# One decoder step on one core: merge loads in rows, matmuls in fours, early sample queries, and seven gates computed ahead

## The chip, the cores and the metric

The kernel runs on one core of one Trainium2 chip, as one program launched once. The metric is the device time in microseconds; lower is better. A core has five engines that run their own instruction streams and wait for each other through semaphores: TensorE (PE, with weight loads shown apart as PEld), VectorE (DVE), ScalarE (ACT), GpSimd (POOL) and SyncE (SP), which in this kernel issues every DMA.

## The reference

One inference step of one decoder layer, for a prompt of 512 tokens and for 8 sample sequences of 4 new tokens each (32 sample tokens; 544 token columns in all), width 1024, everything in float32:

```python
gate, (qa, ka, va, za, qkv_b, zb, a_b, b_b, ga, gb) = layer_front(x, c, w_cond, b_cond, w_in)
# branch A: dilated sliding-window softmax attention, 3 head groups, (window, dilation) =
# (128,1), (512,4), (2048,16), 8 heads of 64 each; the groups' outputs are combined with
# weights = softmax over their log-sum-exp
o_a = combine_groups(outs, lses)
# branch B: causal conv of width 4, silu, l2-normed q and k, gated delta rule in chunks
state, o_b = delta_branch(qkv_ext, a_b, b_b, state0, conv_w, a_log, dt_bias)
# layer_back
ya = o_a.reshape(bsz, seq, A_OUT_WIDTH).astype(dtype) * jax.nn.silu(za)
ob = ob * lax.rsqrt(jnp.mean(ob * ob, axis=-1, keepdims=True) + NORM_EPS) * b_norm_w
yb = ob.reshape(bsz, seq, B_WIDTH).astype(dtype) * jax.nn.silu(zb)
merged = jax.nn.sigmoid(ga) * (ya @ w_branch_a) + jax.nn.sigmoid(gb) * (yb @ w_branch_b)
r = (ALPHA * x + gate[:, None] * (merged @ w_out)).astype(jnp.float32)
# then LayerNorm over each row of r
```

The sample tokens attend to caches of 128, 512 and 2048 positions per sequence. The outputs are both results, the new caches (nearly all of their bytes are copied from the old caches by DMA), the conv states and the delta states.

## The kernel before, in words

**Tiles.** The whole input projection is done in column tiles of 128 output columns. One tile is a *job*: for each half of the 544 token columns (272), 8 blocks of the contraction times three matmuls `hi*hi`, `hi*lo`, `lo*hi`, because every float32 operand is split into a rounded part and a rest. So a job of 8 blocks is 48 matmuls of 128 by 128 by 272. ACT makes `hi` of a weight tile, DVE makes `lo`. Weight tiles are loaded by SP into `wraw` (three buffers), split into `wsp` (two buffers each), and results go to two PSUM banks `pp`. Branch A's output product (`w_ga`) has 4 blocks, so 24 matmuls per job.

**Order of the jobs.** First 60 jobs for the projections of conv/delta-rule heads and attention; then `za_job` 0 to 3 (the gate of branch A's four 128-column groups), `zb_job` 0 to 7 (the gate of branch B's eight heads); then for each of 8 columns `gate_job("gb")` and `branch_job("gb")`, then two `gate_job("ga")`; then for each of 8 columns the rest of `gate_job("ga")` and `branch_job("ga")` with `merge_after`, and last the product with `w_out` and the LayerNorm, five row tiles in two column halves.

**Beside the jobs.** `delta_blocks` and `delta_rule` handle the eight heads of branch B, `prompt_attention` handles the four groups j of branch A. After each odd j it does the *merge*: it gathers the softmax statistics by matmuls into a PSUM bank that another matmul has filled with ones, computes weights `R`, stores `R` to DRAM (`dw`), loads rows of it back broadcast over 64 partitions (`wv`), and for each of two groups multiplies `ya` and `NB` by their weights and adds them. The `wv` tiles use the two buffers of the tag `PT`. For j = 1 these six operations per merge run on POOL (`ce = ge`), for j = 3 on DVE. `sample_attention` is called twice: the early one (`T` = 0) streams its keys and values through nine tiles of the pool `op` (the tag `o`), called `slab`; the late one (`T` = 1) streams through `s2` tiles called `kv`. Each multiplies key tiles by the query rows `qr` and reduces them on DVE, then the same with values. `qr` is made by transposing the sample queries, storing them to DRAM (`qd`) and loading them back in another shape. `sample_delta` updates the sample states. `gate_rows` multiplies the conditioning vector by the last third of `w_cond` and spreads it to `gp` and `gs`, which the last stage multiplies with.

**What sets the order.** The body only records operations with a rank. `schedule()` then simulates the five engines with a table of costs and writes out a fixed order for each engine (list scheduling: lowest rank first among those ready). PE operations of the jobs have rank 9, the last; the jobs' other operations have rank -1, the first. Tiles of a pool are handed out in the order of recording, a tile is handed on when its last operation has been placed, and a pool can only be opened when those before it on its side have been closed, which needs every operation on them placed. Every engine then executes its list strictly in order and waits where an operand isn't there yet. The copies of the caches (`moves`, 168 DMAs of half a megabyte) have due times in that simulation from 48 to 850 us, on SP's list like all other DMAs.

**Pools that matter here.** `ap` holds attention's tiles (`P`, `PT`, `NB`, `spare`, `wv`), `dl` the delta rule's. `zp` (tiles `zt` and `rbo` of `zb_job` and of the gates) opens only after `ap` and `dl` have been closed, so after the last merge and the last head of the delta rule. `op` has 9 tiles: slabs, then `nd`, then the eight `ybh` of branch B, then the four `yal` of branch A. The pool `al` (`gp`, `gs`, `wo`) and `wcp` (the last third of `w_cond`) open after the late sample attention is over.

Of the kernel before, what the change touches and what calls it, by code (L numbers as in the profile page):

```python
# [37 lines left out]
MOVES = (48.0, 850.0)  # L38
S0B = 7
# [203 lines left out]
class Recorder:  # L243
# [439 lines left out]
def body(ctx, tc, io):  # L683
# [49 lines left out]
    bnw = consts.tile([128, 1], F32, name="bnw")  # L733
    hbnw = consts.tile([128, 1], F32, name="hbnw")
    eps4 = consts.tile([128, 1], F32, name="eps4")
    ve.memset(eps4, 4.0 * NORM_EPS)
    eps1 = consts.tile([128, 1], F32, name="eps1")
# [15 lines left out]
    hmask = keep.tile([128, 4], F32, name="hmask")  # L753

# [572 lines left out]
    dw = dram.tile([2, 128, 2, 128], F32, name="dw")  # L1327
# [32 lines left out]
    def prompt_attention():  # L1360

        for j in range(4):
# [95 lines left out]
            pe.matmul(pt, ones[0:1, :], ones[0:1, None, :].to_broadcast([1, 4, 128]), start=True, stop=True)  # L1458
# [20 lines left out]
            sp.dma_start(dw[j // 2], R[:, 0:2])  # L1479
            ce = ve if j == 3 else ge  # L1480
            for j2 in (j - 1, j):
                wv = []
                for u in range(2):
                    w = ap.tile([128, 512], F32, name="wv", tag="PT", bufs=2)
                    for hh in range(2):
                        h4 = 2 * (j2 % 2) + hh
                        sp.dma_start(w[64 * hh:64 * hh + 64].rearrange("p (r c) -> p r c", r=4),
                                     dw[j // 2, h4:128:32, u, :][None].to_broadcast([64, 4, 128]))
                    wv.append(w.rearrange("p (r a n) -> p r a n", r=4, a=4))
                time = lambda t: t[:, :SEQ].rearrange("p (n a r) -> p r a n", a=4, r=4)  # L1490
                ce.tensor_mul(time(ya[j2]), time(ya[j2]), wv[0])
                ce.tensor_mul(time(NB[:, j2 % 2]), time(NB[:, j2 % 2]), wv[1])
                ce.tensor_add(ya[j2][:, :SEQ], ya[j2][:, :SEQ], NB[:, j2 % 2])
                threads.set(merged[j2], 0.0)
# [55 lines left out]

    def sample_attention(T, t, stream, W, pace_of, by, over):
# [11 lines left out]
        qn = stream()[0:64, 0:256]  # L1563
        for jl in range(2):
            j = 2 * T + jl
            pt = pg()
            pe.transpose(pt[0:96, 0:128], ks[:, j].rearrange("p g n -> p (g n)"), ident)
            pe.transpose(pt[0:96, 128:256], vs[:, j].rearrange("p g n -> p (g n)"), ident)
            pe.transpose(pt[0:64, 256:384], qs[:, j, 1:3].rearrange("p g n -> p (g n)"), ident)
            ve.tensor_copy(knv[:, :, 128 * jl:128 * jl + 128], pt[0:96, 0:256].rearrange("p (u c) -> p u c", u=2))  # L1570
            se.activation(qn[:, 128 * jl:128 * jl + 128], pt[0:64, 256:384], AF.Copy)
        sp.dma_start(qd[T].rearrange("g t c -> (g t) c"), qn)

        qr = t["qr"].rearrange("p (g d) -> p g d", g=2)
        sp.dma_start(qr, qd[T].rearrange("g t (h d) -> (t h) g d", d=64))
# [81 lines left out]
        for x, vt in enumerate(vts):  # L1657
            for y in range(m):
                bp, bl = (m * x + y) // 2, (m * x + y) % 2
                o = pO[32 * bp:32 * bp + 32, 0:256]  # L1660
# [3 lines left out]
                pe.matmul(o, PTa[:, 128 * bl + 32 * bp:128 * bl + 32 * bp + 32], vt[:, 256 * y:256 * y + 256],  # L1664
                          start=False, stop=(bl == 1), tile_position=(0, 32 * bp))
# [24 lines left out]
    def early_tiles():  # L1690

        slab = [op.tile([128, NT], F32, name="slab", tag="o") for _ in range(9)]
        t = {}
        for i, names in ((4, ("Sa", "qr")), (5, ("Sb", "od", "o2")), (6, ("sba", "PTn")), (7, ("sbb", "om")), (8, ("knv",))):
# [4 lines left out]
        for n in ("Qz", "PTa", "sst"):  # L1699
# [135 lines left out]
    def zb_job(h):  # L1835
# [3 lines left out]
        def begin():  # L1839
            t["rows"] = zp.tile([128, SEQ], F32, name="rbo")  # L1840
            sp.dma_start(t["rows"], dO[h])

        def evac(n, ps):
            if not n:
                t["zt"] = zp.tile([128, NT], F32, name="zt")
# [4 lines left out]
        def after():  # L1850
# [9 lines left out]
        return column_job(("zb", h), evac=evac, begin=begin, after=after)  # L1860
# [11 lines left out]
    def gate_job(s, m):  # L1872

        def evac(n, ps):
            if not n:
                gate_tile[s, m] = zp.tile([128, NT], F32, name="zt")
# [17 lines left out]
    def gate_rows():  # L1894

        def load(part):
            for n in range(2):
                for k in range(0, KT, 2):
                    wc = wcp.tile([128, 2, 512], F32, name="wc")
                    sp.dma_start(wc, cond_rows(part, k, 2)[:, :, 512 * n:512 * n + 512])  # L1900
                    yield k, n, wc[:, 0]
                    yield k + 1, n, wc[:, 1]

# [5 lines left out]
        for _ in cond_product(2, load, ps):  # L1909
            yield 1.0  # L1910
# [21 lines left out]
    jobs += [za_job(j) for j in range(4)] + [zb_job(h) for h in range(8)]  # L1932
# [12 lines left out]
    threads.add(stream(60 + 4), 9)  # L1945
# [9 lines left out]
    def early():  # L1955
        yield freed[1], merged[1]
        yield from sample_attention(0, *early_tiles(), 512, 6.0, (ve,), early_over)
# [23 lines left out]
    def samples():  # L1981
# [3 lines left out]
        yield from sample_attention(1, {n: s1.tile([128, w], F32, name=n) for n, w in SHAPES.items()},  # L1985
# [12 lines left out]
    jobs += [gate_job("ga", m) for m in range(2)]  # L1998
# [44 lines left out]
    for m in range(8):  # L2043
        jobs += [gate_job("ga", m)] * (m > 1) + [branch_job("ga", m, 4, of_a, after=merge_after(m))]
# [188 lines left out]
```

## Time and profile before

| | |
|---|---|
| time, median of 3 runs | 1012.84 us |
| the three runs | 1013.37, 1012.84, 1010.07 us |
| the profiled execution's own time | 1010.26 us |
| its span, first to last instruction | 1008.3 us |
| TensorE clock granted, mean over the span | 0.973 |
| ACT busy | 418.4 us (41%) |
| POOL busy | 80.1 us (8%) |
| DMA read and written | 220.40 MB and 103.93 MB |

All of the kernel's arithmetic is recorded through one helper, so every row says line 630; rows are told apart by tile names (`pp<-hhi,hi` is a matmul of a job into its PSUM bank, `lo<-wt,hi` the split of a weight tile on DVE). A PE row's duration includes the pipeline's depth, so matmuls that follow each other every 0.125 us show 0.29 us each. "Idle before" counts only time in which that engine did nothing.

### The profile page before, as it was taken

Reading aid. Unit: us, or ns where it says so; the run is one execution under the profiler, and the core shown is the slowest. Engines: PE = TensorE matmul, PEld = TensorE weight load, DVE = VectorE, ACT = ScalarE, POOL = GpSimd, SP = SyncE. Lnnn points to the kernel's source line nnn. Section 1 sums busy time; section 2 is a strip of 40 time slices with the busy share of each in tenths; the row PEclk is TensorE's granted clock in tenths of the full one; section 3 lists DMA queues with packets and bytes.
Section 4 is the critical chain, followed back from the end, with each engine's and each line's share of the span. In section 5 each row is a group of like instructions: output and inputs, shape, how many; then the busy total and the mean of one; then the engine's idle time right before and its main releaser. Section 6 shows DMA issues by size and latency. Waiting matters only on the chain.

```text
span 1008.3 us, 20686 instructions
## 1 busy us (share of the span) xinstructions
PE 939.0 (93%) x8074; PEld 850.1 (84%) x8074; DVE 736.7 (73%) x1612; ACT 418.4 (41%) x975; POOL 80.1 (8%) x182
## 2 busy tenths in 40 slices
PE   4899999999999989999999999959999999799896
PEld 1699989999889988878898988848999998578785
DVE  0574576767599888989998776447978999546468
ACT  0364348444565443557434564223332221225220
POOL 0120001100102600011000101010010000000000
PEclk9899999999999999999999999879999999799998
DMA  9677755676787888857778474496889999824312
GB/s 361 194 243 226 228 176 202 203 242 182 219 272 259 264 274 272 288 189 247 244 278 280 155 221 151 138 283 254 275 263 392 422 394 328 308 85 135 130 56 108
DMA packets 109605, 237.98 MB, mean 236 GB/s; under 512 B 30899, under 2 KB 66429, under 8 KB 106821
## 3 DMA queue, kind: packets, MB, share of 16 engines
q1 hardware_dynamic: 109508, 236.68, 69.9%
q8 instruction: 63, 1.03, 0.4%
q14 instruction: 34, 0.27, 0.1%
HBM read 220.40 MB, written 103.93 MB: 322 GB/s over the span
## 4 chain that ended last, share of the span: by engine, by line
PE 47%; DVE 20%; DMA 6%; issue 3%; ACT 2%; POOL 0%; SPq 0%; DVEq 0%; ACTq 0%; POOLq 0%
PE pp L630 35%; PE pg L630 6%; PE pd L630 5%; DVE lo L630 2%; DVE r L630 2%; DVE slab L630 2%; DMA wv<-dw 2%; DVE acc L630 2%; PE pb L630 1%; DVE tmp L630 1%; DVE Tb L630 1%; DVE NTs L630 1%; DMA slab<-in_ks 1%; DMA wt<-in_w_in 1%; ACT hi L630 1%
## 5 line engine op out<-in xcount | busy, mean ns | idle before, releaser
L630 PE MATMUL pp<-hhi,hi 128*128 128x272 f32 x1408 | 416.1, 296 | 14.3 <-DVE zt L630 10.7
L630 PE MATMUL pp<-hhi,lo 128*128 128x272 f32 x1408 | 415.7, 296 | 0.6 <-DVE lo L630 0.6
L630 PE MATMUL pp<-hlo,hi 128*128 128x272 f32 x1408 | 413.7, 294 | 1.4 <-DVE hlo L630 1.4
L630 PEld LDWEIGHTS pp<-hhi,hi 128*128 128x128 f32 x1408 | 269.4, 191 | 18.8 <-DVE zt L630 11.2
L630 PEld LDWEIGHTS pp<-hlo,hi 128*128 128x128 f32 x1408 | 269.5, 191 | 5.1 <-issue 2.6
L630 PEld LDWEIGHTS pp<-hhi,lo 128*128 128x128 f32 x1408 | 269.2, 191 | 3.9 <-issue 1.9
L630 ACT ACTIVATE hi<-wt 128x1024 fp32r<-128x1024 f32 (+1 forms) x104 | 106.7, 1026 | 180.6 <-PE pp L630 164.2
L630 DVE TENSOR_TENSOR lo<-wt,hi 128x1024 fp32r<-128x1024 f32 (+1 forms) x104 | 124.1, 1193 | 66.4 <-ACT hi L630 65.9
L630 DVE SCALAR_TENSOR_TENSOR acc<-ext,cw,acc 128x568 f32<-128x568 f32 x72 | 57.5, 799 | 1.3 <-ACT ecum L630 0.8
L630 ACT ACT_TABLE_LOAD x38 | 48.8, 1283 | 13.9 <-DMA cT<-in_cT 7.8
L630 DVE TENSOR_TENSOR slab<-slab 128x512 f32<-128x512 f32 (+1 forms) x66 | 43.7, 676 | 3.1 <-DMA slab<-in_ks 2.6
L630 DVE TENSOR_REDUCE slab<-slab 128x8 f32<-128x512 f32 (+1 forms) x64 | 42.5, 674 | 0.3
L630 ACT ACTIVATE P<-P,st 128x256 f32<-128x256 f32 (+1 forms) x64 | 31.3, 490 | 24.5 <-DVE st L630 24.1
L630 ACT ACTIVATE zt<-pp 128x272 f32<-128x272 f32 x48 | 18.5, 388 | 52.9 <-PE pp L630 38.7
L630 PE MATMUL pp<-ybl,hi 128*128 128x272 f32 x128 | 37.1, 290 | 0.0
L630 PE MATMUL pp<-ybh,hi 128*128 128x272 f32 x128 | 36.8, 287 | 0.0
L630 PE MATMUL pp<-ybh,lo 128*128 128x272 f32 x128 | 36.8, 287 | 0.0
L630 PE MATMUL pg<-k,q 64*128 64x128 f32 (+1 forms) x192 | 33.3, 329 | 1.9 <-DVE st L630 1.9
L630 POOL COPY cx<-ext 128x3 f32<-128x3 f32 (+1 forms) x48 | 26.7, 586 | 84.2 <-ACT ext L630 84.2
L630 DVE SCALAR_TENSOR_TENSOR zt<-zt,pp 128x272 f32<-128x272 f32 x32 | 13.7, 433 | 26.1 <-PE pp L630 20.6
L630 PEld LDWEIGHTS pg<-k,q 64*128 64x128 f32 x192 | 22.4, 186 | 9.0 <-issue 3.6
L630 DVE CUSTOM_DVE_ANT_0 P<-pg,bias 128x256 f32<-128x256 f32 (+1 forms) x64 | 24.3, 400 | 7.4 <-PE pg L630 7.1
(398 smaller groups left out, 1617.0 us busy)
## 6 DMA issues: line engine op xcount, KB each, us to landing
out_kv_s<-in_cache SPq DMA_DIRECT2D x144, 512.0 KB
wt<-in_w_in SPq DMA_DIRECT2D x88, 512.0 KB
out_kv_s<-in_cache SPq DMA_DIRECT2D x24, 496.0 KB
wc<-in_w_cond SPq DMA_DIRECT2D x8, 1024.0 KB
slab<-in_ks SPq DMA_DIRECT2D x32, 256.0 KB
slab<-in_vs SPq DMA_DIRECT2D x32, 256.0 KB
kv<-in_ks SPq DMA_DIRECT2D x16, 512.0 KB
kv<-in_vs SPq DMA_DIRECT2D x16, 512.0 KB
```

The source lines that it names most:

```text
L630: getattr(real[x.engine], x.name)(*map(arg, x.args), **{k: arg(v) for k, v in x.kw.items()})
```

## The change

1. **Merge.** The bank of ones is written by DVE (`memset`) and not by a matmul. `R` goes to `dw` with four DMAs of four partitions each, so that a head's 512 weights lie in one row; each `wv` load then reads 2 KB rows and not 512-byte pieces. The second group's `wv` tiles take the two buffers of the tag `P`, not the same two as the first group's. The arithmetic of both merges runs on DVE.
2. **Orders in fours.** In `schedule()`, the first operation of a group recorded `together` now waits for all that any operation of the group needs from outside. The matmuls of the sample attention's last product are recorded in such a group, by fours in four different column strips of PE; those of `gate_rows` in groups of four contraction blocks with their loads recorded in front.
3. **Early sample queries.** `sample_queries` (transposes, copies, store and load of `qd`) is taken out of `sample_attention`. For `T` = 0 it is called right before; for `T` = 1 it is called at the end of the early thread, once the last attention inputs are there, into the kept tile `qr1`. Four one-column tiles become one, and `sst` moves to a slab, which makes room for `qr1`.
4. **Gates ahead.** `zb_job` 0 and 1 are put between `za_job` 1 and 2, with their `zt` in `op` tiles; the rest of their work (`finish`: the rows from DRAM, transposes, scaling, split) is done at the beginning of the next stage by `finish_early`. And `gate_job("ga")` 2 to 6 are added behind 0 and 1, ahead of the end of the stage, with `zt` in `op` tiles.

```diff
+EARLY_A, EARLY_B = 7, 2
...
+        for op in ops:
+            if op.group is not None and op.n != op.group[0]:
+                for d, data in op.deps.items():
+                    if d < op.group[0]:
+                        first = ops[op.group[0]].deps
+                        first[d] = first.get(d, False) or data
...
-    dw = dram.tile([2, 128, 2, 128], F32, name="dw")
+    dw = dram.tile([2, 4, 2, 4, 128], F32, name="dw")
...
-            pe.matmul(pt, ones[0:1, :], ones[0:1, None, :].to_broadcast([1, 4, 128]), start=True, stop=True)
+            ve.memset(pt, 1.0)
...
-            sp.dma_start(dw[j // 2], R[:, 0:2])
-            ce = ve if j == 3 else ge
+            for r in range(4):
+                sp.dma_start(dw[j // 2, :, :, r, :], R[32 * r:32 * r + 4, 0:2])
...
-                    w = ap.tile([128, 512], F32, name="wv", tag="PT", bufs=2)
+                    w = ap.tile([128, 512], F32, name="wv", tag="PT" if j2 < j else "P", bufs=2)
                     for hh in range(2):
-                        h4 = 2 * (j2 % 2) + hh
-                        sp.dma_start(w[64 * hh:64 * hh + 64].rearrange("p (r c) -> p r c", r=4),
-                                     dw[j // 2, h4:128:32, u, :][None].to_broadcast([64, 4, 128]))
+                        src = dw[j // 2, 2 * (j2 % 2) + hh, u].rearrange("r c -> (r c)")
+                        sp.dma_start(w[64 * hh:64 * hh + 64], src[None, :].to_broadcast([64, 512]))
...
+    def sample_queries(T, qn, qr):
+
+        for jl in range(2):
+            pt = pg()
+            pe.transpose(pt[0:64, 0:128], qs[:, 2 * T + jl, 1:3].rearrange("p g n -> p (g n)"), ident)
+            se.activation(qn[:, 128 * jl:128 * jl + 128], pt[0:64, 0:128], AF.Copy)
+        sp.dma_start(qd[T].rearrange("g t c -> (g t) c"), qn)
+        sp.dma_start(qr.rearrange("p (g d) -> p g d", g=2), qd[T].rearrange("g t (h d) -> (t h) g d", d=64))
...
+        with rec.together():
+            for bp in range(4):
                 bs = slice(32 * bp, 32 * bp + 32)
-                if not bl:
-                    pe.matmul(o, PTn[0:96, bs], knv[:, 1, :], start=True, stop=False, tile_position=(0, 32 * bp))
...
+                t["zt"] = op.tile([128, NT], F32, name="zt", tag="o") if early else zp.tile([128, NT], F32, name="zt")
...
+        if early:
+            unfinished.append((rows, finish))
+            return column_job(("zb", h), evac=evac)
+        return column_job(("zb", h), evac=evac, begin=rows, after=finish)
+
+    def finish_early():
+        for rows, finish in unfinished:
+            rows()
+            yield 3.0
+            finish()
...
+                far = s == "ga" and 2 <= m < EARLY_A
+                gate_tile[s, m] = op.tile([128, NT], F32, name="zt", tag="o") if far else zp.tile([128, NT], F32, name="zt")
...
+            for k0 in range(0, KT, 4):
+                wc = []
+                for k in (k0, k0 + 2):
+                    wc.append(wcp.tile([128, 2, 512], F32, name="wc"))
+                    sp.dma_start(wc[-1], cond_rows(2, k, 2)[:, :, w])
+                with rec.together():
+                    take(cond_product(2, lambda part: ((k0 + k, n, wc[k // 2][:, k % 2]) for k in range(4)), ps), 99)
+                yield 2.0
...
-    jobs += [za_job(j) for j in range(4)] + [zb_job(h) for h in range(8)]
+    jobs += [za_job(j) for j in range(2)] + [zb_job(h, True) for h in range(EARLY_B)] + [za_job(j) for j in range(2, 4)]
+    jobs += [zb_job(h) for h in range(EARLY_B, 8)]
...
+        t, slabs = early_tiles()
+        sample_queries(0, slabs()[0:64, 0:256], t["qr"])
+        yield from sample_attention(0, t, slabs, 512, 6.0, (ve,), early_over)
+        yield tuple(ready[3, g] for g in range(3))
+        sample_queries(1, slabs()[0:64, 0:256], qr1)
...
-    jobs += [gate_job("ga", m) for m in range(2)]
+    jobs += [gate_job("ga", m) for m in range(EARLY_A)]
+    threads.add(finish_early(), 0)
...
-        jobs += [gate_job("ga", m)] * (m > 1) + [branch_job("ga", m, 4, of_a, after=merge_after(m))]
+        jobs += [gate_job("ga", m)] * (m >= EARLY_A) + [branch_job("ga", m, 4, of_a, after=merge_after(m))]
```

More of the change, by code (lines that the diff above doesn't have):

```diff
@@ L732, in body @@
     ve.memset(ones, 1.0)
-    bnw = consts.tile([128, 1], F32, name="bnw")
-    hbnw = consts.tile([128, 1], F32, name="hbnw")
-    eps4 = consts.tile([128, 1], F32, name="eps4")
+    small = consts.tile([128, 4], F32, name="small")
+    bnw, hbnw, eps4, eps1 = (small[:, i:i + 1] for i in range(4))
     ve.memset(eps4, 4.0 * NORM_EPS)
-    eps1 = consts.tile([128, 1], F32, name="eps1")
     ve.memset(eps1, NORM_EPS)
@@ L753, in body @@
     hmask = keep.tile([128, 4], F32, name="hmask")
+    qr1 = keep.tile([128, 128], F32, name="qr1")
     def cond_product(part, load, ps):
@@ L1656, in sample_attention @@
         m = W // 256
[L1657 to L1660, printed above, removed]
+        with rec.together():
+            for bp in range(4):
                 bs = slice(32 * bp, 32 * bp + 32)
-                if not bl:
-                    pe.matmul(o, PTn[0:96, bs], knv[:, 1, :], start=True, stop=False, tile_position=(0, 32 * bp))
-                pe.matmul(o, PTa[:, 128 * bl + 32 * bp:128 * bl + 32 * bp + 32], vt[:, 256 * y:256 * y + 256],
-                          start=False, stop=(bl == 1), tile_position=(0, 32 * bp))
+                pe.matmul(pO[bs, 0:256], PTn[0:96, bs], knv[:, 1, :], start=True, stop=False, tile_position=(0, 32 * bp))
+            for bl in range(2):
+                for bp in range(4):
+                    x, y = divmod(2 * bp + bl, m)
+                    pe.matmul(pO[32 * bp:32 * bp + 32, 0:256], PTa[:, 128 * bl + 32 * bp:128 * bl + 32 * bp + 32],
+                              vts[x][:, 256 * y:256 * y + 256], start=False, stop=(bl == 1), tile_position=(0, 32 * bp))
         om = t["om"].rearrange("p (h d) -> p h d", h=4)
@@ L1693, in early_tiles @@
         t = {}
-        for i, names in ((4, ("Sa", "qr")), (5, ("Sb", "od", "o2")), (6, ("sba", "PTn")), (7, ("sbb", "om")), (8, ("knv",))):
+        for i, names in ((4, ("Sa", "qr", "sst")), (5, ("Sb", "od", "o2")), (6, ("sba", "PTn")), (7, ("sbb", "om")), (8, ("knv",))):
             at = 0
@@ L1698, in early_tiles @@
                 at += SHAPES[n]
-        for n in ("Qz", "PTa", "sst"):
+        for n in ("Qz", "PTa"):
             t[n] = s0.tile([128, SHAPES[n]], F32, name=n)
@@ L1833, in za_job, with zb_job, rows @@
         return column_job(("za", j), evac=evac, after=after, start=(merged[j],))
-    def zb_job(h):
+    unfinished = []
+    def zb_job(h, early=False):
         t = {}
-        def begin():
+        def rows():
             t["rows"] = zp.tile([128, SEQ], F32, name="rbo")
@@ L1848, in evac, with finish @@
             ve.scalar_tensor_tensor(half(zt, n), half(zt, n), 1.0, ps, op0=OP.add, op1=OP.mult)
-        def after():
+        def finish():
             zt, pt = t["zt"], pg()
@@ L1894, in gate_rows @@
     def gate_rows():
[L1896 to L1902, printed above, removed]
         b = io["b_cond"][:, 2 * D:]
@@ L1908, in gate_rows @@
         yield 4.0
-        for _ in cond_product(2, load, ps):
-            yield 1.0
         for n in range(2):
             w = slice(512 * n, 512 * n + 512)
+            for k0 in range(0, KT, 4):
[6 more added lines that the diff above has]
+                yield 2.0
             Y = zp.tile([128, 512], F32, name="Y", tag="rbo")
@@ L1984, in samples @@
         s1 = pool(sctx1, "s1", 1)
-        yield from sample_attention(1, {n: s1.tile([128, w], F32, name=n) for n, w in SHAPES.items()},
+        yield from sample_attention(1, {n: qr1 if n == "qr" else s1.tile([128, w], F32, name=n) for n, w in SHAPES.items()},
                                     lambda: s2.tile([128, D], F32, name="kv", tag="cache"), 1024, 2.0, (ve,), late_over)
```

17 lines of the change are left out of this document (4 added, 13 removed).

## The prediction

> **What bounds the kernel now.** I read the page first, then windows of PE, then PE's timeline with its idle times, then the chain of work that ended last.
>
> ```profile
> PE 939.0 (93%) x8074; PEld 850.1 (84%) x8074; DVE 736.7 (73%) x1612; ACT 418.4 (41%) x975; POOL 80.1 (8%) x182
> ...
> PE   4899999999999989999999999959999999799896
> ```
> ```profile
> 656.69 8.16 DMA wv<-dw
> ...
> 667.75 5.81 PE pp L630 x24
> ...
> 747.51 57.28 PE pp L630 x457
> ...
> 863.00 5.39 PE pp L630 x20
> ```
>
> PE is the bound, busy 93% of the span; some 69 us are without it. The second fence is the chain, with start, length and count: a job's matmuls follow every 57.28 / 457 = 0.125 us, so a job of 48 costs 6.0 us. Besides the first two slices and the end, two slices stand out, the 27th (PE 5) and the 35th (PE 7). So the question is what PE waits for in those two places.
>
> ```profile
> 649.60 0.29 PE L630 MATMUL pp<-hhi,lo 128*128 128x272 f32 x1
> ...
> 667.75 0.60 PE L630 MATMUL pp<-hhi,hi 128*128 128x272 f32 x1 [10.67 <-DVE zt L630]
> ```
> ```profile
> 650.00:660.00 10.00, 5.00 (x20) 3.69 (x20) 6.20 (x10) 6.24 (x15) 0.00 (x0) 0.83 0.69 204
> 660.00:670.00 10.00, 2.25 (x10) 2.25 (x11) 5.87 (x12) 0.00 (x0) 3.04 (x5) 0.51 0.87 271
> ```
> ```profile
> 664.88 1.02 DVE L630 TENSOR_TENSOR NB<-NB,wv 128x512 f32<-128x512 f32 x1 [3.29 <-DMA wv<-dw]
> 665.93 0.69 DVE L630 TENSOR_TENSOR ya<-ya,NB 128x512 f32<-128x512 f32 x1
> 666.65 0.69 DVE L630 SCALAR_TENSOR_TENSOR ya<-ya,spare 128x512 f32<-128x512 f32 x1
> ```
>
> **Gap one** is the last merge. At 649.7 PE has finished `za` 0 to 3 and holds both halves of `zb` 0 in the two PSUM banks; they can only be evacuated into a `zt` of `zp`, and that pool opens after `ap` is done, so after the merge. The merge loads `wv` in two rounds, the second issued only when the first has freed the tiles, and the last load takes 8.16 us. The two window rows (length, then busy us of PE, PEld, DVE, ACT, POOL, then granted clock, DMA share and GB/s) show PE busy 5.00 and 2.25 of 10 us: 12.75 us lacking, and the clock down to 0.51. The first 24 matmuls then take 5.81 us and not 3.0: 2.8 us more. The small ones before, 5 us at a clock of 0.83, lose about 1. Price: 16.6 us.
>
> ```profile
> 851.91 0.40 PE L630 MATMUL pg<-kv,PTa 128*32 128x256 f32 x1
> ```
> ```profile
> 860.93 0.45 PE L630 MATMUL pg<-cst,o 128*128 128x128 f32 x1 [6.06 <-DVE o L630]
> 863.00 0.82 PE L630 MATMUL pp<-yah,hi 128*128 128x272 f32 x2 [1.61 <-ACT yah L630]
> ```
> ```profile
> 747.00:763.00 16.00, 16.00 (x130) 16.00 (x129) 7.29 (x10) 4.26 (x9) 0.00 (x0) 1.00 0.88 297
> 763.00:852.00 89.00, 89.00 (x757) 87.37 (x757) 86.38 (x92) 21.29 (x36) 0.00 (x0) 1.00 0.99 384
> 863.00:947.00 84.00, 80.98 (x534) 68.54 (x534) 38.09 (x61) 26.78 (x47) 0.00 (x0) 0.95 0.45 149
> ```
>
> **Gap two** is the end of the late sample attention. DVE is full from 763 to 852 (86.38 of 89). PE runs out of jobs at 851.9, does the short product, and waits for DVE: 6.06 + 1.61 = 7.7 us, and 20 matmuls in 5.39 and not 2.5 us: 2.9. Price: 10.6 us.
>
> **The change, part by part.**
>
> *Two early `zb` jobs.* 96 matmuls, 12.0 us of PE, move from behind gap one into it, and the next job's halves can still be held in the banks as now. PE then runs dry at 649.7 + 12.0 + some 4 us of the delta rule's small matmuls = 665.7. Their `zt` need `op` tiles:
>
> ```profile
> L630 DVE TENSOR_TENSOR slab<-slab x66: 224/680/1175, 276.7 to 553.6; 128x512 f32<-128x512 f32 x64, 128x64 f32<-128x64 f32 x1, 128x128 f32<-128x128 f32 x1
> ```
> ```profile
> L630 SPq DMA_DIRECT2D wv<-dw x16: 574/613/1220, 321.4 to 656.7; - x16
> L630 SPq DMA_DIRECT2D dw<-R x2: 326/330/334, 317.2 to 641.0; - x2
> ```
>
> The slabs are last used near 554, a hundred us earlier; free. `finish` issues the same instructions later.
>
> *Merge loads.* `R` is stored from 641.0. Four stores cost SP 4 x 0.33 us in place of one, 1 us more, and eight `wv` loads 8 x 0.61 = 4.9 us in one run, since the second group no longer waits. The last is issued near 649 and with the 8.2 us of now lands near 657.4. Then 1.02 + 0.69 + 0.69 = 2.4 us: the merge ends at 660, and `zp` opens 7 us earlier than now and 5 before PE runs dry. I take 16.0 of the 16.6 us. The lower end is 6: DVE waits in order for a late `wv`, and the `lo` of the early jobs stands behind it. What is late next is the delta rule's last head: its pool `dl` has to close as well.
>
> The sum uses no faster landing. The Trainium skill ("DMA: Bandwidth & Descriptors", section "Why small descriptors are slow (HBM only)") counts about 3 extra cycles per packet, 32 bytes a cycle: by it 2 KB rows in place of 512 bytes save an estimated 12% of the moving time (67 cycles against 76), nothing of the queueing. No row here separates the two.
>
> *Ones.*
>
> ```profile
> 630.87 1.12 PE L630 MATMUL pg<-ones 1*128 1x512 f32 x2
> 636.57 0.69 DVE L630 COPY R<-pg 128x512 f32<-128x512 f32 x1 [3.52 <-PE pg L630]
> ```
>
> Two merges lose this step, 1.12 us less the overlap with its neighbours, 1.05 each: -2.1. The `memset` on DVE has no row; it lies between nothing and that copy's 0.69, taken as 0, because DVE idles 3.52 us before the copy.
>
> *First merge on DVE.*
>
> ```profile
> 325.00:350.00 25.00, 25.00 (x199) 24.88 (x198) 20.80 (x37) 9.48 (x20) 17.71 (x14) 1.00 0.79 252
> 350.00:375.00 25.00, 21.40 (x157) 20.85 (x156) 21.50 (x60) 11.35 (x32) 1.42 (x5) 0.93 0.83 279
> ```
> ```profile
> 349.16 1.60 POOL L630 TENSOR_TENSOR ya<-ya,NB 128x512 f32<-128x512 f32 x1
> ```
> ```profile
> 349.55 2.30 DVE L630 TENSOR_TENSOR lo<-wt,hi 128x1024 fp32r<-128x1024 f32 x1
> ```
> ```profile
> L630 DVE TENSOR_TENSOR lo<-wt,hi 128x1024 fp32r<-128x1024 f32 x96 | 118.6, 1235 | 66.2 <-ACT hi L630 65.7
> ```
>
> DVE gets 2 x (1.02 + 1.02 + 0.69) = 5.5 us more. It is free 4.2 and 3.5 us in these windows, so the work fits; and the `lo` at 349.55, beside POOL's addition, took 2.30 us and not 1.235, which goes. But DVE now waits for `wv` itself, and queued behind it are the `lo` PE needs. Ends: -5 (the 3.6 us PE lacks in 350 to 375, with the low clock after) to +8 (DVE waiting as long as one of its loads takes now, 8.16 us, with nothing beside it). The cover argues for the middle: +1.
>
> *Early sample queries.*
>
> ```profile
> 754.51 0.45 SPq L630 DMA_DIRECT2D qr<-qd  x1
> ```
> ```profile
> 760.84 1.22 DVE L630 TENSOR_TENSOR kv<-kv,qr 128x1024 f32<-128x1024 f32 x1
> ```
>
> The first key product waits for `qr`, fetched at 754.5. With `qr1` in place it can start near 754, some 7 us earlier; DVE is idle 8.7 of the 16 us before 763. That is DVE's gain, and PE's only if DVE ends last. The same four transposes, two copies and two DMAs run earlier, while SP has pauses.
>
> *Five gates ahead.* 5 x 6.0 = 30 us move in front of gap two. PE comes to the end of its jobs at 851.9 - 16.6 + 30 = 865.3, and with the short product at 868. DVE's chain, now over by 862.5 (the first `yah` matmul follows at 863.00), gains 7 us and at least part of gap one, and gets five `lo`, 5 x 1.235 = 6.2 us: at worst, with no gain at all, it ends at 868.7 and `yah` follows at 870. So between 0 and 2 us of waiting are left, and 10.6 us go; lower end 7.
>
> *The last stage* keeps eight branch jobs and one gate. PE's 80.98 us become 80.98 - 30 - 2.9 = 48, DVE's 38.09 - 6.2 = 32. The transfers, 149 GB/s x 84 us = 12.5 MB, fall into some 52 us: 240 GB/s, below the 384 of the row above. But within eight adjacent branches DVE is as full as PE:
>
> ```profile
> 902.26 0.44 DVE L630 SCALAR_TENSOR_TENSOR zt<-zt,pp 128x272 f32<-128x272 f32 x1 [0.60 <-PE pp L630]
> 902.73 0.72 DVE L630 TENSOR_TENSOR zt<-zt,mT 128x544 f32<-128x544 f32 x1
> 903.38 0.69 DVE L630 TENSOR_TENSOR lo<-wt,hi 128x512 fp32r<-128x512 f32 x1
> 904.18 0.72 DVE L630 TENSOR_TENSOR mlo<-zt,mhi 128x544 fp32r<-128x544 f32 x1
> ```
>
> 2 x 0.44 + 0.72 + 0.69 + 0.72 = 3.0 us, and a short `ms`, against 24 x 0.125 = 3.0 of PE: no slack, and some 0.2 us over in each of eight, taken as +2 (0 to 8, if a weight tile or a pair of `wc` is late each time). The fours change nothing I can price: `gate_rows` already spreads its matmuls over four strips, and the sample product lies before a DVE chain. 0, down to -2.
>
> **Sum**, against the profiled execution's own 1010.26 us (span 1008.3 and 2.0 around it): 1010.3 - 16.0 - 10.6 - 2.1 + 1 + 2 = 984.6, so **985**. The median of the runs shown is 2.6 above that execution; the range has room for it.
>
> **The rivals.**
>
> *A. DVE's waits keep gap one* (chance 0.15). DVE's last `NB` waits 3.29 us for `wv` in its list; if the `lo` of the early jobs stand behind such waits, PE starves with work in sight and 10 of the 16 us stay: 995. For it: DVE runs strictly in order, and now all four waits come close together. Against it: the early jobs' weights can be split before the merge begins.
>
> *B. Transfers bound the sample stage* (0.10). Its DMA share is 0.99. Five gates bring their weight tiles, 128 x 1024 x 4 bytes each, 2.6 MB more, 6.8 us at 384 GB/s, and if the sample chain ends last it ends that much later: 992. Against it: DVE shows almost no wait for `kv` there. The Trainium skill ("DMA: Bandwidth & Descriptors", section "Where 436 GB/s comes from") gives about 358 GB/s as one core's share of HBM; the row's 384 is above that, so it doesn't hold as a ceiling here.
>
> *C. The early jobs don't land in the gap* (0.06): the planner, with its own costs, puts them after it. Then gap two alone closes: 1010.3 - 10.6 - 2.1 + 2 = 1000.
>
> *D. Slower* (0.07): both merges block DVE for long. The planner counts on short landings of 2 KB rows and puts DVE's products early; the loads really stand behind half-megabyte cache copies on the one SP queue. Each merge then costs PE the extra wait w plus 2.8 us of low clock; 2 x (w + 2.8) passes the 28.7 us of gains from w = 12, so from landings of some 20 us, 8.2 now. With w = 16: 1010.3 + 37.6 - 28.7 = 1019.
>
> **How the numbers follow.** Forecast 0.62 (978 to 991), A 0.15, B 0.10, C 0.06, D 0.07. The range takes the forecast, B, A and C's 1000, and downward the lower ends of the first merge, the fours and the last stage (984.6 - 6 - 2 - 2): 974 to 1001. About 0.3% (3 us) is what a measurement of this kernel can tell from no change. Faster 0.87; within it 0.06 (tails of A and C); slower 0.07 (D).
>
> **What would show it.** Right: PE's window around the last merge is full and the clock 1.0, `zt` evacuations of two jobs stand before the last `NB<-NB,wv`; PE runs through from about 640 to 870 without an idle of over 2 us; POOL has no `ya` or `NB`. Wrong: an idle of PE before `lo` with DVE waiting for `wv`; `kv` products waiting for DMA; a new gap in the branch stage or around 330 to 350.

## The result, and the profile after

The changed kernel takes 987.05 us, the median of 4 runs (984.89 to 987.92), where the kernel before took 1011.46 us beside it (4 runs, 1009.06 to 1013.37): a ratio of 0.976, with a 95% interval of 0.972 to 0.980. The profiled execution took 984.89 us, its span is 982.8 us, the granted clock 0.98. The forecast was 985 (974 to 1001). Of all executions of the runs below, one, the profiled one of `old_merge_loads`, took 2407.8 us where the three others of that kernel took 994.87 to 997.23; it is not used.

The page after: busy time, then PE's busy tenths and its clock in 40 slices.

```profile
PE 922.8 (94%) x8070; PEld 842.9 (86%) x8070; DVE 739.4 (75%) x1620; ACT 413.6 (42%) x971; POOL 75.7 (8%) x176
...
PE   4899999999999999999999799998999999999896
...
PEclk8799999999999999999999999998999999999998
```

The two holes of before (27th and 35th slice) are gone or nearly so: an 8 is left in the 28th. There is a new 7, the 23rd slice, and the forecast did not have it. The span fell by 25.5 us. PE's busy time fell by 16.2 of these (939.0 to 922.8) and its idle time by 9.3 (69.3 to 60.0).

Windows of the changed kernel (length, then busy us of PE, PEld, DVE, ACT, POOL, then granted clock, DMA share, GB/s), and one of the kernel before that was not shown yet:

```profile
325.00:350.00 25.00, 23.11 (x181) 22.39 (x180) 25.00 (x45) 12.25 (x31) 11.16 (x10) 1.00 0.88 268
350.00:375.00 25.00, 22.53 (x231) 21.57 (x230) 22.14 (x63) 9.55 (x24) 0.42 (x2) 1.00 0.85 284
375.00:400.00 25.00, 23.50 (x216) 21.48 (x214) 24.05 (x68) 9.57 (x17) 0.77 (x3) 1.00 0.62 187
545.00:575.00 30.00, 23.28 (x226) 20.77 (x225) 23.81 (x64) 17.61 (x49) 3.15 (x11) 0.89 0.57 190
...
650.00:660.00 10.00, 10.00 (x84) 10.00 (x83) 4.99 (x10) 5.43 (x15) 0.00 (x0) 1.00 0.61 188
660.00:670.00 10.00, 7.37 (x50) 7.14 (x50) 9.41 (x15) 4.86 (x8) 2.06 (x4) 0.83 0.84 268
...
763.00:852.00 89.00, 88.51 (x757) 87.77 (x756) 83.19 (x88) 23.96 (x40) 0.00 (x0) 1.00 0.97 381
850.00:875.00 25.00, 25.00 (x211) 23.11 (x211) 12.14 (x21) 8.06 (x15) 0.00 (x0) 1.00 0.86 303
```
```profile
545.00:575.00 30.00, 29.36 (x313) 25.13 (x312) 23.86 (x51) 17.80 (x42) 4.69 (x10) 1.00 0.59 204
```

Read stage by stage: **gap two** has closed, 850 to 875 is full at full clock. **Gap one** lacks 2.63 us where it lacked 12.75. In 325 to 350 DVE is now full, 25.00 of 25, and PE lacks 1.89 us and 2.47 more in the next window. And in **545 to 575** PE lacks 6.72 us, where before it lacked 0.64, with the clock at 0.89 where it was 1.00. So about 18 us of idle went and 8 to 9 came back.

What is left of gap one, in the timelines of PE and of DVE of the changed kernel:

```profile
667.29 0.59 PE L638 MATMUL pp<-hhi,hi 128*128 128x272 f32 x1 [2.63 <-DVE spare L638]
```
```profile
660.23 1.04 DVE L638 TENSOR_TENSOR ya<-ya,wv 128x512 f32<-128x512 f32 x1
...
666.21 0.68 DVE L638 TENSOR_TENSOR orow<-pd,rn 128x512 f32<-128x512 f32 x1
666.81 0.43 DVE L638 SCALAR_TENSOR_TENSOR spare<-spare,pp 128x272 f32<-128x272 f32 x1
```

No product waits for `wv` any more. But the products of both groups and the row of the delta rule stand in DVE's list from 660.23 to 666.8 in front of the `spare` that empties a PSUM bank, and PE waits for that bank.

Now the new gap. DVE's timeline of the changed kernel, PE's after it, and DVE's of the kernel before:

```profile
558.35 0.35 DVE L638 SCALAR_TENSOR_TENSOR z<-pd,rc,vr 128x128 f32<-128x128 f32 x1 [0.58 <-PE pd L638]
558.61 3.34 DVE L638 RECIPROCAL kq<-kq 128x512 f32<-128x512 f32 x1
561.87 1.23 DVE L638 SCALAR_TENSOR_TENSOR KQ<-ext,acc 128x512 f32<-128x512 f32 x2
```
```profile
562.99 0.59 PE L638 MATMUL pp<-hhi,hi 128*128 128x272 f32 x1 [2.32 <-ACT ext L638]
```
```profile
559.91 0.69 DVE L630 SCALAR_TENSOR_TENSOR KQ<-ext,acc 128x512 f32<-128x512 f32 x1
...
568.60 3.35 DVE L630 RECIPROCAL kq<-kq 128x512 f32<-128x512 f32 x1
```

In both kernels DVE takes 3.34 us for the reciprocal of the sample preparation. Before, it comes after the last `KQ`. Now it comes ahead of two of them; `KQ` frees the buffer `ext`, ACT can only then empty PE's banks into `ext`, and PE waits 2.32 us at 562.99. Before that it has waits of 1.75, 1.29, 0.44 and 0.46 us for DVE and ACT in the delta rule's chain, because no job's matmul can be done meanwhile. PE's list differs from that of the kernel before from about 115 us on: an edit makes the planner order everything anew that comes behind the first place where it matters.

### The profile page after: what moved, and what is told of

The parts are those of the page before. It is cut to its first block, busy times and chain, and to the rows that moved or that the text cites. A ratio compares the mean times of both kernels' runs of the same rounds, so it can differ in the third digit from the quotient of the medians.

```text
span 982.8 us, 20665 instructions
## 1 busy us (share of the span) xinstructions
PE 922.8 (94%) x8070; PEld 842.9 (86%) x8070; DVE 739.4 (75%) x1620; ACT 413.6 (42%) x971; POOL 75.7 (8%) x176
## 5 line engine op out<-in xcount | busy, mean ns | idle before, releaser
L638 DVE TENSOR_REDUCE slab<-slab 128x8 f32<-128x512 f32 (+2 forms) x66 | 42.5, 656 | 0.6 <-ACT slab L638 0.4
L638 POOL COPY cx<-ext 128x3 f32<-128x3 f32 (+1 forms) x48 | 32.4, 704 | 90.8 <-ACT ext L638 90.6
L638 ACT ACTIVATE ext<-pp 128x272 f32<-128x272 f32 (+2 forms) x72 | 20.0, 315 | 23.2 <-PE pp L638 19.3
```

Source lines behind the costliest of these rows:

```text
L638: getattr(real[x.engine], x.name)(*map(arg, x.args), **{k: arg(v) for k, v in x.kw.items()})
```

## The experiments

**The four parts, one at a time, and a new order with no edit.** Theory: each part is worth what its term in the sum says. Rival: the parts cover each other. A second rival for all readings: a new order alone moves the time.

The twelve runs come from three sessions of four runs each, in the order in which they stand here. The kernel before took 1008.88, 1007.06 and 1009.94 us in them, where it took 1011.46 beside the changed kernel. So a difference of two times from different sessions can be off by some 2 to 4 us. The ratio, given with each run, is to the kernel before of its own session; where it tells something else than the times, the text says so.

Branch A's gates 2 to 6 back behind gap two:

```diff
-EARLY_A, EARLY_B = 7, 2
+EARLY_A, EARLY_B = 2, 2
```

> The changed kernel, with branch A's gates 2 to 6 back beside their branch jobs (two gates ahead, as before) and all else kept; only the order after the delta rule differs. Theory (gates fill gap two): the sample chain now ends some 7 us earlier, gap two reopens for what is left: PE runs out of jobs near 835 and waits up to 30 us less that gain; idle of PE of 10 to 25 us between 830 and 870 ahead of yah, and a time of 997 to 1005. Rival (the early queries and the shorter merge alone had closed it, the gates are not needed): no idle over 2 us there and 987. Another rival (adjacent branches starve on DVE and the gates ahead cost the last stage something): a time below 987.

Measured: 999.62 us (997.31 to 1002.06), ratio 0.989 (0.982 to 0.995). Two windows of it:

```profile
763.00:852.00 89.00, 83.26 (x718) 80.57 (x716) 83.13 (x89) 21.47 (x37) 0.00 (x0) 0.98 0.97 375
850.00:875.00 25.00, 18.87 (x120) 16.26 (x121) 14.38 (x29) 7.70 (x13) 0.00 (x0) 0.75 0.96 332
```

Gap two is back, from about 835 on, 5.74 + 6.13 us without work and a clock of 0.75 after it. DVE's order is that of the changed kernel up to 838, so this is a clean difference: five gates ahead are worth 12.6 us in this place (13 by the ratios).

No `zb` job ahead of the merge:

```diff
-EARLY_A, EARLY_B = 7, 2
+EARLY_A, EARLY_B = 7, 0
```

> The changed kernel with none of branch B's z jobs computed ahead of the merge; merge loads, queries and gates kept. Theory (the two jobs are the 12 us of work that covers the merge): PE is without work for about 12 us more between 640 and 670, and some low clock with it, 999 to 1003. Rival (the faster merge alone closes most of gap one): 987 to 992. The order differs from PE's row at about 540 us on, so the gap at 554 to 570, which the changed kernel has and the kernel before has not, may come or go too: without it the time is about 8 us less than either.

Measured: 993.55 us (992.93 to 994.78), ratio 0.983 (0.978 to 0.988), so between the two. PE's timeline:

```profile
668.12 0.79 PE L638 MATMUL pd<-z,XF 128*128 128x128 f32 x2 [2.51 <-DVE z L638]
...
675.68 0.39 PE L638 MATMUL pp<-hhi,hi 128*128 128x272 f32 x1 [2.95 <-DVE zt L638]
```

Only some 5 us more of idle, not 12: without the two jobs PE does the delta rule's small products in the stretch. Two jobs of 6.0 us are worth some 6.5 us here (7.5 by the ratios), not 12; the order is a new one from 537 on, and the control below moves the time nearly as far.

The merge's weights as before (one store, short rows, one pair of tiles):

```diff
-dw = dram.tile([2, 4, 2, 4, 128], ...)
+dw = dram.tile([2, 128, 2, 128], ...)
...
-    w = ap.tile([128, 512], F32, name="wv", tag="PT" if j2 < j else "P", bufs=2)
+    w = ap.tile([128, 512], F32, name="wv", tag="PT", bufs=2)
```

> The changed kernel with the merge's weights stored and loaded as before: one store, 512-byte rows, and the second pair of weight tiles waiting for the first; both merges still on DVE, the memset kept. Theory (the second round of loads is what made the merge late): the last merge ends 5 to 7 us later, PE idles that much longer around 665 to 675, and the first merge holds DVE longer: 993 to 1000. Rival (with the early z jobs the loads are covered anyway): 985 to 989.

Measured: 995.11 us, the median of three (994.87 to 997.23), ratio 0.985 (0.979 to 0.991): 8 us more (9.5 by the ratios). That speaks for the theory that the early jobs do not cover the loads. There is no profile of this kernel to read; the mechanism is read from `pool_old_loads` below.

The control: the changed kernel with other due times for the cache copies.

```diff
-MOVES = (48.0, 850.0)
+MOVES = (48.0, 846.0)
```

> The changed kernel with nothing changed but the due times of the cache copies, spread up to 846 in place of 850, so that the planner orders the whole kernel anew. It measures how far a new order alone moves the time. Theory (the stages that the change does not touch scatter by some us with every new order): 982 to 994, with other idle places than the changed kernel's, the gap at 554 to 570 among those that may be gone. Rival (the time is set by the edits alone): 986 to 988 and the same gaps.

Measured: 980.34 us (979.95 to 983.62), ratio 0.971 (0.965 to 0.976). This is below the theory's range. So a new order with the same work is 6.7 us faster than the changed kernel by the times, 5 us by the ratios. That is the size of what cannot be put down to an edit when two of these kernels are compared by their times alone; one control shows that it can be as large, not that it is never larger. The gap at 545 to 575 is there too (PE 22.27 of 30), so this new order did not remove it, and the next four runs look for its cause.

**The new gap.** Theory one: the long reciprocal in front of `KQ`. Theory two: the first merge on DVE made it. Theory three: an accident of the order, which belongs to no part.

The reciprocal in four pieces:

```diff
-        ve.reciprocal(kqf, kqf)
+        for i in range(2):
+            for c in (0, 128):
+                ve.reciprocal(kqf[:, i, c:c + 128], kqf[:, i, c:c + 128])
```

> The changed kernel with the one reciprocal of 128 x 512 in the sample preparation (3.34 us on DVE at 558.6) cut into four of 128 columns, so that the KQ of the last head can pass between them. Theory (this reciprocal in front of KQ is what empties PE between 554 and 570): DVE reaches the two KQ after 1.7 us and not 3.3, PE gains 1.5 to 4 us in 545 to 575: 981 to 986. Rival (PE starves there because the delta rule of the head before is late and still holds the KQ tile, the reciprocal only fills DVE's wait): no change in that window, 985 to 989.

Measured: 983.10 us (980.39 to 986.56), ratio 0.976 (0.971 to 0.981), which is the ratio of the changed kernel. PE has 25.82 of 30 us in 545 to 575, 2.5 more; two of the four pieces still stand ahead of `KQ`. But not all of the 2.5 us is the reciprocal's: PE's wait that `KQ` ends is 1.21 us and not 2.32, and the rest comes from waits in the delta rule's chain ahead of the pieces. The gain doesn't reach the end: at 670.2 PE waits 3.73 us for a `zt`, where the changed kernel waits 2.63 in that stage.

The first merge's arithmetic on POOL:

```diff
+                ce = ve if j == 3 else ge
-                ve.tensor_mul(time(ya[j2]), time(ya[j2]), wv[0])
+                ce.tensor_mul(time(ya[j2]), time(ya[j2]), wv[0])
...
```

> The changed kernel with the first merge's products and sum on POOL again, the last merge on DVE. Two terms hang on it. The first merge on DVE was put at +1 (-5 to +8): by windows the stretch 300 to 450 holds PE about equally busy with either. And in this order the sample preparation stands behind the last KQ: theory (the gap at 554 to 570 comes from the order that the planner found once the first merge was on DVE): the window 550 to 575 is full as in the kernel before (24.4 of 25 us), 977 to 981. Rival (the gap has another cause, the early z jobs or the merge's loads): the gap stays and the time is 985 to 990.

Measured: 974.22 us (972.94 to 976.64), ratio 0.967 (0.963 to 0.972): below the theory's own range by the time, 8 us below the changed kernel by the ratios. Its windows:

```profile
325.00:350.00 25.00, 24.77 (x196) 24.46 (x195) 23.68 (x33) 10.46 (x21) 17.44 (x14) 1.00 0.89 299
350.00:375.00 25.00, 24.14 (x187) 23.29 (x187) 23.97 (x67) 11.81 (x34) 1.58 (x4) 1.00 0.81 251
375.00:400.00 25.00, 24.11 (x289) 21.25 (x290) 21.52 (x47) 7.43 (x15) 1.16 (x3) 1.00 0.90 308
545.00:575.00 30.00, 28.80 (x310) 26.26 (x309) 23.99 (x48) 23.02 (x57) 4.61 (x12) 1.00 0.59 191
```

The gap of 545 to 575 is gone, and from 325 to 375 PE lacks 1.09 us where the changed kernel lacks 4.36. But the kernel before, with that merge on POOL too, lacks 3.60 there by the rows in the prediction. So the price of the first merge on DVE lies between 0.8 and 3.3 us by these windows.

The sample product in its old order, and the product of ones in place of the `memset`:

```diff
-        with rec.together():
-            for bp in range(4):
+        for x, vt in enumerate(vts):
+            for y in range(m):
...
```

> The changed kernel with the sample product of the attention in its old order (strip by strip, not held together). The fours were put at 0, down to -2. In this order, too, the sample preparation stands behind the last KQ. Theory (the gap at 554 to 570 is an accident of one order and belongs to no part of the change): the window 550 to 575 is full or nearly so, 977 to 982, the product itself within 1 us of the same length. Rival (the gap belongs to the first merge on DVE, which is kept here): the gap stays, 985 to 989; if the fours themselves save something, up to 2 us more.

```diff
-            ve.memset(pt, 1.0)
+            pe.matmul(pt, ones[0:1, :], ones[0:1, None, :].to_broadcast([1, 4, 128]), start=True, stop=True)
```

> The changed kernel with the product of ones in both merges again in place of the memset. The step was put at 2 x 1.05 us on PE. In this order, too, the sample preparation stands behind the last KQ. Theory (accident of the order): the gap at 554 to 570 goes, 6 to 9 us, and the two products bring 1 to 2 us back: 979 to 983. Rival (the gap stays): 986 to 990.

Measured: `no_fours` 980.96 us (979.89 to 982.02), ratio 0.974 (0.969 to 0.978); `ones_matmul` 979.09 us (978.22 to 980.02), ratio 0.972 (0.968 to 0.976). Both put something back that costs PE time and are no slower: by the times 6 and 8 us faster than the changed kernel, by the ratios 2 and 4, which is within the control's size. Both lose the gap, with the first merge still on DVE. So theory two falls: the first merge on DVE does not by itself bring the gap. The window 545 to 575 of all thirteen kernels that can be read, sorted by one fact of DVE's list, whether the (first) reciprocal stands ahead of the last head's last `KQ`:

| reciprocal | kernels, PE busy of 30 us |
|---|---|
| ahead | after 23.28, no_gates_ahead 23.29, no_early_zb 22.74, moves_control 22.27, pool_old_loads 22.56; in four pieces, split_prep 25.82 |
| behind | before 29.36, before_gates 29.35, first_merge_pool 28.80, pool_three_zb 28.82, no_fours 29.11, pool_late_queries 28.42, ones_matmul 28.30 |

The two sets do not touch. The gap goes with the order, and the order is not tied to one part: `pool_old_loads` has it with the first merge on POOL, `no_fours` is without it with the merge on DVE. That is theory three.

The reciprocal is the mark of that order, but only the smaller part of the price. In `pool_old_loads` it is over at 556.4, and `KQ` still waits, for PE's last product of the head before, which reads the old `KQ`:

```profile
560.80 1.29 DVE L638 SCALAR_TENSOR_TENSOR KQ<-ext,acc 128x512 f32<-128x512 f32 x2 [0.51 <-PE pd L638]
```

PE's wait that `KQ` ends is 1.21 or 1.22 us where `KQ` waits for that product (`split_prep`, `no_early_zb`, `pool_old_loads`) and 2.32 us in the changed kernel, where the reciprocal stands right in front. So the reciprocal costs about 1.1 us. The rest, as the traces read, is that PE's jobs are ahead of the delta rule: in the changed kernel ACT empties a bank into `ext` at 546.9, and the next time, after `KQ`, at 562.5. `ones_matmul` comes to these `KQ` hardly earlier, at 559.3, but its jobs fill `ext` until 554.8, and it has no gap. Why the planner lists it so was not followed further.

**The parts on a base without that gap, and a better version.** First the gates alone on the kernel before, then three edits of `first_merge_pool`.

```diff
+EARLY_A = 7
...
-    jobs += [gate_job("ga", m) for m in range(2)]
+    jobs += [gate_job("ga", m) for m in range(EARLY_A)]
...
```

> The kernel before with one part of the change alone: five more of branch A's gates ahead of the samples' end, their tiles in the freed slabs; gap one, merges and queries stay as before. The order up to the delta rule's end is that of the kernel before. Theory (30 us of ready work cover gap two): no idle of PE over 1 us between 850 and 900, the clock full there, and 10.6 us less: 996 to 1000 where the kernel before has 1007 to 1009 beside it. Rival (without the early queries and the shorter gap one DVE's chain ends too late): 3 to 5 us of gap two stay, 1000 to 1004.

Measured: 993.37 us (990.88 to 995.45), ratio 0.984 (0.981 to 0.987): a larger gain than the theory's range. Gap two is closed to the last:

```profile
850.00:875.00 25.00, 25.00 (x204) 23.26 (x204) 15.90 (x22) 7.12 (x12) 0.00 (x0) 1.00 0.89 319
```

PE's last stage, from the first `yah` matmul to the first of the output product, takes 36.9 us where 79.4 - 30 - 2.9 = 46.5 were to be expected. Half of the difference is that 20 of the 32 `wc,cs` matmuls now come ahead of it; the other 4.8 us are won. So the gates bring 16 us by themselves, about a third of it behind gap two.

```diff
+        if T:
+            sample_queries(1, stream()[0:64, 0:256], t["qr"])
...
-        sample_queries(1, slabs()[0:64, 0:256], qr1)
```

> The changed kernel with the first merge on POOL, as in first_merge_pool (974.2), and the second half's sample queries made inside the sample attention again. Theory (with seven gates ahead DVE's chain no longer sets PE's end, so the early queries are worth little): the key products start some 7 us later, DVE's chain ends up to 7 us later, and PE waits 0 to 3 us ahead of yah: 974 to 979. Rival (they are what lets the chain end in time): idle of 5 us or more before yah and 980 to 985.

Measured: 985.99 us (982.16 to 988.29), ratio 0.976 (0.972 to 0.980). That is a little above the rival's time, with a wait only a little above the theory's:

```profile
877.61 0.30 PE L638 MATMUL pg<-cst,o 128*128 128x128 f32 x1 [1.66 <-DVE o L638]
879.52 0.53 PE L638 MATMUL pp<-yah,hi 128*128 128x272 f32 x2 [1.61 <-ACT yah L638]
```

The first key product of the late half starts at 777.75 where `first_merge_pool` has 732.03, and DVE's chain ends last again: 3.3 us of waiting. The other 8 or 9 us (5 by the ratios) lie earlier: PE reaches its first branch B matmul at 734.6 and not at 725.3, in an order that is a new one from 547 on, with idle places before 720. No run here shows whether these hang on the queries.

```diff
-dw = dram.tile([2, 4, 2, 4, 128], ...)
+dw = dram.tile([2, 128, 2, 128], ...)
...
```

> The changed kernel with the first merge on POOL (974.2) and the merges' weights stored and loaded as before: one store, 512-byte rows, the second pair of weight tiles waiting for the first pair. Theory (the second round of loads makes the last merge some 5 to 7 us later, and the two early z jobs do not cover that): PE's idle around 665 grows from 2.7 to 7 to 10 us, with a low clock after: 980 to 986. Rival (covered): 973 to 977. In old_merge_loads the same edit cost 9 us on the changed kernel.

Measured: 987.31 us (985.89 to 989.24), ratio 0.978 (0.976 to 0.981), a little above the theory's range. DVE's timeline, then PE's:

```profile
666.19 1.04 DVE L638 TENSOR_TENSOR ya<-ya,wv 128x512 f32<-128x512 f32 x1 [3.52 <-DMA wv<-dw]
670.24 1.02 DVE L638 TENSOR_TENSOR NB<-NB,wv 128x512 f32<-128x512 f32 x1 [3.01 <-DMA wv<-dw]
```
```profile
673.02 0.80 PE L638 MATMUL pd<-S,KQ 128*128 128x128 f32 x2 [6.02 <-DVE S L638]
...
681.82 0.59 PE L638 MATMUL pp<-hhi,hi 128*128 128x272 f32 x1 [3.14 <-DVE zt L638]
```

This is rival A of the prediction, seen at work. DVE waits in its list for the second pair of loads; behind it stands the `S` of the delta rule's last head, and PE waits 6.02 us for that and then 3.14 for the pool of `zt`. Against the 2.65 us of `first_merge_pool` that is 6.5 us of idle; this order also has the gap of 545 to 575 (22.56 of 30 where `first_merge_pool` has 28.80), which makes up the rest of the 13 us (11 by the ratios).

```diff
-EARLY_A, EARLY_B = 7, 2
+EARLY_A, EARLY_B = 7, 3
```

> The changed kernel with the first merge on POOL (974.2) and three of branch B's z jobs ahead of the merge in place of two. The order is the same up to about 640 us. Theory (what is left of gap one, 2.65 us of idle and a low clock after it, is ready work that is lacking): PE runs through 650 to 675 with a full clock and the time falls by 3 to 6 us: 968 to 971. Rival (DVE's queue at the merge holds the evacuations whatever work there is): the same idle at 666, 973 to 976, or more where a third job's lo and zt stand in front of the merge.

Measured: 968.16 us (967.27 to 968.82), ratio 0.959 (0.957 to 0.962), faster than both kernels, 18.9 us below the changed one. The order is that of `first_merge_pool` up to about 640:

```profile
660.00:670.00 10.00, 9.81 (x76) 9.49 (x75) 6.69 (x15) 5.07 (x9) 3.92 (x8) 1.00 0.81 255
```
```profile
665.84 0.39 PE L638 MATMUL pp<-hhi,hi 128*128 128x272 f32 x1 [0.19 <-DVE spare L638]
```

A third job of 6.0 us took the time down by 6.1 (8 by the ratios). In the traces PE begins its branch B matmuls 6.4 us earlier (718.9, 725.3 in `first_merge_pool`). So the rest of gap one, 2.65 us of idle and the low clock behind it, was a lack of ready work; the other two or three us were won between there and branch B and were not traced one by one.

## Why the prediction was right, step by step

The time and the forecast agree to 2 us, and the two gaps were the right places. But several terms were off by 4 to 8 us, and that they cancelled is luck.

- **Gap one, -16.0.** Idle fell from 12.75 to 2.63 us, 10.1 less. Of the 3.8 us that the prediction counted for the low clock, 2 or more stayed: after the wait 16 matmuls took 3.99 us and not 2.0. So some 11.5 of the 16 us came. The places were right: `zt` of the two jobs stands from 620.6 to 652.5, PE's time up to the gap (664.7) was put at 665.7. The step that failed is the merge's end, put at 660. `R` was stored 9 us later than before, because prompt attention ended later in the new order; the four stores cost SP not 0.33 but 0.70 us each,

```profile
649.83 2.80 SPq L638 DMA_DIRECT2D dw<-R  x4
```

  and the merge's last addition ended at 666.3, where it ended at 666.6 before: not 7 us earlier, but at the same time. So PE's idle fell because two jobs lay in that stretch and because the loads made up for the late `R`. Taken away, the loads are worth 8 us (`old_merge_loads`; 6.5 us of waiting can be seen in `pool_old_loads`), the early jobs 6.5; with three jobs the wait of 2.65 us goes.
- **Gap two, -10.6.** All of it went. DVE had even more room than the working said: `yah` is ready from about 862, PE comes to it at 877.74.
- **The last stage, +2: wrong.** PE's first matmul of the stage and its first of the output product, in the changed kernel and then the latter in the kernel before:

```profile
877.74 0.29 PE L638 MATMUL pp<-yah,hi 128*128 128x272 f32 x1
...
915.80 0.40 PE L638 MATMUL pp<-wo0h,ms 128*64 128x512 f32 x1
```
```profile
942.40 0.40 PE L630 MATMUL pp<-wo0h,ms 128*64 128x512 f32 x1
```

  From 863.00 to 942.4 were 79.4 us, now it is 38.1. Less the 30 of the gates and the 2.9 of low clock, 8.4 us went that the sum did not have. By steps from start to start, 3.8 of them are `wc,cs` (2.8 by the fours, 1.0 moved ahead), and the other 4.6 are 2.2 of idle (PE idles 0.3 us there in all, where it idled 2.5) and, for the rest, low clock (0.94 over the stage before, 1.00 now). The claim "no slack, and some 0.2 us over in each of eight" did not come true. `before_gates` shows nearly the same, 4.8, without the other parts.
- **The fours, 0 down to -2: mis-sized.** Groups of PE, busy us and mean ns, before and after:

```profile
L630 PE MATMUL pd<-wc,cs 128*32 128x512 f32 x32 | 7.2, 606 | 0.0
L630 PE MATMUL pg<-slab,PTa 128*32 128x256 f32 x16 | 3.3, 380 | 0.0
L630 PE MATMUL pg<-kv,PTa 128*32 128x256 f32 x16 | 3.0, 382 | 0.0
L630 PE MATMUL pg<-slab 96*32 96x256 f32 x8 | 2.3, 391 | 0.0
L630 PE MATMUL pg<-knv,PTn 96*32 96x256 f32 x8 | 2.3, 391 | 0.0
```
```profile
L638 PE MATMUL pd<-wc,cs 128*32 128x512 f32 x32 | 4.3, 605 | 0.0
L638 PE MATMUL pg<-slab,PTa 128*32 128x256 f32 x16 | 1.7, 385 | 0.6 <-DMA slab<-in_cache 0.6
L638 PE MATMUL pg<-kv,PTa 128*32 128x256 f32 x16 | 1.0, 379 | 0.0
L638 PE MATMUL pg<-slab 96*32 96x256 f32 x8 | 0.6, 391 | 0.0
L638 PE MATMUL pg<-knv,PTn 96*32 96x256 f32 x8 | 0.6, 391 | 0.0
```

  One matmul is as long as before, but four lie beside each other in time: 8 of 391 ns take 0.6 us and not 2.3. Groups overlap, so the gain is counted by the steps from one start on PE to the next: 14.4 us to 7.5, so -6.9, 2.8 of it in `wc,cs` and mostly inside the last stage. The prediction put them at nothing, since `gate_rows` already spread its matmuls over four strips. But in these runs matmuls lie beside each other only where those for different strips also follow each other in PE's list. The kernel without the sample product's fours shows the old length again; by steps its sample product takes 7.0 us and not 3.5, where its own theory had put them within 1 us:

```profile
L638 PE MATMUL pg<-slab,PTa 128*32 128x256 f32 x16 | 3.8, 385 | 0.0
```

  The Trainium skill ("TensorEngine Tiling (Array Packing)", section "Theoretical Speedup") gives up to four times for a dimension of 32; the groups of 96 rows reach it here, 2.3 to 0.6.
- **Ones, -2.1.** The two products (2.2 us busy) are gone from the changed kernel's groups, and the `memset` took 0.485 us on DVE, inside the 0 to 0.69 that it was given. `ones_matmul` confirms the product's cost only in its groups; its time is below the changed kernel's, as the gap of 545 to 575 is not in it.

```profile
L638 PE MATMUL pg<-ones 1*128 1x512 f32 x4 | 2.2, 640 | 0.0
```

- **First merge on DVE, +1: not settled within its range.** It did not come by the way that was feared, a wait for `wv` (there is none). "So the work fits" held only just: DVE is full from 325 to 350 (25.00 of 25). Windows put it between +0.8 and +3.3. Of the kernels without the late gap, the one with this merge on POOL (974.2) is 5 to 7 us below those with it on DVE (979.1 and 981.0), which is no more than the control moved. Inside -5 to +8, and more likely above +1 than below.
- **Not in the sum: the new order.** This is the step that failed most. The gap of 545 to 575 is 6.1 us more of idle (6.72 less 0.64) and a clock of 0.89 over 30 us, which is up to 3.3 us more: some 7 to 9. It was listed as a sign ("a new gap"), without a price and for other places. The sum took every stage that the diff does not touch as unchanged; the control moved by 5 to 6.7 us with no edit but the due times of copies.
- **Early queries.** The key products start at 735.4, put at 754; with seven gates ahead PE waited for nothing there. On the base of `first_merge_pool`, which reaches that place earlier, they spare 3.3 us of waiting.
- **Rivals.** B did not come: 381 GB/s, a DMA share of 0.97, PE full. The Trainium skill's share of about 358 GB/s ("DMA: Bandwidth & Descriptors", section "Where 436 GB/s comes from") did not bound this stage after the change either. C did not come. D needed landings of 20 us; no product of a merge in the changed kernel waited for one.

So the sum by what was measured: about -11.5 and -10.6 for the gaps, -2.1 for the ones, -6.9 for the fours, -4.6 more in the last stage; against them +1 to +3 for the first merge, some +7 to +9 for the new gap, and 2.4 us more of idle before 300 (PE busy 277.76 us there, 280.12 before). That is -21 to -25, where the span shows -25.5; the difference was not found. These terms are read from one execution of each kernel, and single ones may be off by 1 or 2 us.

## What to carry to other kernels

Where a list scheduler writes out the order, an edit changes stages that it does not touch: make one run with a null edit that forces a new order, and take its difference as the least that a time can prove; below that, compare windows. A free share of an engine does not say that work fits: look at what stands behind the new work in the list when the engine is full. And ready work put in front of a wait is worth its length only as far as nothing else was going to fill that wait; two jobs of 6.0 us were worth 6.5 us, not 12.

## What the runs showed of the hardware that was not expected

A short wait was enough for a low clock. After the single idle of 2.63 us at 667.29 the chain of waits of the changed kernel has

```profile
667.29 3.99 PE pp L638 x16
```

so 0.25 us for each matmul where 0.125 is usual, and the window of 660 to 670 has a granted clock of 0.83. The Trainium skill ("TensorE: Matmul & The Clock Gate", section "HAM oscillation — how this bites in real kernels") warns of gaps of PE over about 3.4 us; this one was shorter, and the price came all the same.
